# Layer 1's sweep of a hybrid encoder: two units of the gate branch ordered ahead of the recurrence gates, and the last small stores and first row loads re-queued

## The chip, the cores and the metric

The kernel runs on one core of one Trainium2 chip. The metric is device time in microseconds (us) of one execution, as the median of several runs; the profile is that of one more execution. A core has a matrix engine (PE, with its weight loads shown as PEld), a vector engine (DVE), a scalar engine for activation functions (ACT), a general engine (POOL), and a queue engine (SP) that does nothing here but issue transfers (DMA) between the chip's memory and the on-chip memory. Each engine executes its own instructions in a fixed order; an instruction whose operands are not there yet holds up all that stand behind it on that engine. POOL can issue transfers too.

## What is computed

Two layers over 2048 rows of 1024 features. Layer 0 mixes windowed attention and a gated MLP; layer 1 is a bidirectional gated linear recurrence. Only layer 1 is touched:

```
xr, g = split(h @ w_in, 2)                 # 1024 -> 2 x 1024
xr = centred_depthwise_conv(xr, conv_w, conv_b)
y  = rg_lru(xr, ..., reverse=False) + rg_lru(xr, ..., reverse=True)
y  = y * silu(g)
x  = layer_norm(ALPHA * x + gate * (y @ w_out), ln_g, ln_b)

def rg_lru(x, w_a, b_a, w_x, b_x, lam, reverse):
    rec_gate, in_gate = sigmoid(x @ w_a + b_a), sigmoid(x @ w_x + b_x)   # per head, 128 x 128
    log_a = -8 * rec_gate * softplus(-lam)
    a, b = exp(log_a), sqrt(1 - exp(2 * log_a)) * in_gate * x
    h[i] = a[i] * h[i-1] + b[i]            # a scan along the rows, forward or backward
```

## The kernel before

Rows are cut into `NT` = 4 tiles of `C` = 512. All products are made to full float32 accuracy from two halves of each operand, a rounded one and its remainder (`split`, lines 154 and 155: ACT rounds, DVE subtracts), so each product of a 128 x 128 weight block with 512 columns is three matmuls (`mm3`, lines 158 to 160).

**The sweep over the tiles, t = 0 to 3.** For each tile the 1024 recurrence channels and the 1024 gate-branch channels are treated in two halves, s = 0 and 1, of four groups g of 128 channels. For one half:

- `x_job` makes the input branch: `job1` runs `job_cm` over 8 units (a unit is one slice of 128 input features, whose weights are one transfer of 512 KB into a buffer `hl`, eight of which exist), 4 groups x 3 matmuls each, 96 matmuls in all, into 4 PSUM banks `pj` of 5. ACT copies the four results into `X` (line 897).
- `build1(t+1)`, in the second half only, builds the next tile's input (DVE transposes, ACT, DVE, POOL).
- `front` makes, for each group, the convolution on DVE (lines 944 and 947), its split, four gate products of three matmuls into PSUM banks `pm` (weights `hg`, line 953), the activations on ACT, and the scans on DVE (lines 994, 1007, 1014).
- `g_job` makes the gate branch: again 8 units, 96 matmuls, into 4 banks `pj`, copied by ACT (line 918).
- `back` multiplies the two. For t < 3 its results go to memory as rows `a_d`, `b_d`, `f_d`, `g_d`, `u_d`, `v_d`, since the backward scan of a tile needs the tile behind it. For t = 3 they are used at once (`y3`), and the first two columns of each group are stored to `y_d` (line 1040, 8 stores in all), because they belong to the tile before.

**The seam.** After the sweep, the output product of tile 3 is made from `y3`: `part_out` (96 matmuls for each half n of the output columns) into all eight PSUM banks, `ps3`. Meanwhile `load_y(2)` fetches the stored rows of tile 2 and finishes its backward recurrence, eight slices k: for even k the tiles `at`, `bt`, `ft`, `gt` (line 1106), a scan (1113), a sum on POOL (1117), a product (1118); for odd k `ut`, `vt` and one or two corrections by the carry `cr` (1127); then the split into `hi` and `lo` that PE multiplies. The two columns from `y_d` are loaded into the same tiles (line 1130). `residual_tile` loads four tiles `z` of 512 KB, the residual rows of tile 3 (line 1144); line 1164 adds `ps3` to them, which frees the PSUM banks for tile 2's output product, and `finish` normalises them (`norm_rows`, lines 614 to 624). Tiles 1 and 0 follow in the same way.

The loads of the seam go into tiles of the pool `outp`, which is laid over the pool `rnn` of the sweep (`ra`, `T`, `ii`, `G`, `hg`): a load waits for the last use of whatever lay in its place. In a pool, tiles are placed in the order in which they are first allocated. SP issues all of these loads and, before the change, the `y_d` stores. In the program each transfer of SP's queue also waits until the one eight places before it has landed.

**What sets the order.** The text of the program is not the order on the engines: a planner orders each engine's instructions beforehand. At any moment it takes, among the instructions whose operands it believes ready, the one that comes first in the text (evictions marked `high_priority` first of all). The order that it finds is then fixed.

Of the kernel before, what the change touches and what calls it, by code (L numbers as in the profile page):

```python
# [17 lines left out]
D = 1024  # L18
KD = D // 128
C = 512  # L20
NT = S // C
# [8 lines left out]
NEL = 5  # L30
PE_FROM = 14
XH = 1
XB = 2


# [18 lines left out]
def kernel(  # L54
# [27 lines left out]
    nc = tc.nc  # L82
# [5 lines left out]
    store = nc.sync.dma_start  # L88
# [24 lines left out]
    y_d = dram.tile([128, KD, 2], F32, name="y_d")  # L113
# [125 lines left out]
    for i in range(2):  # L239
        nc.gpsimd.dma_start(out=vrow0[24 + 8 * i:32 + 8 * i].rearrange("k (a q) -> k a q", a=4),  # L240
                            in_=ada_b[1, i * D:i * D + D].rearrange("(a k q) -> k a q", a=4, q=32))
# [4 lines left out]
    ps = bank(px, "px")  # L246
# [22 lines left out]
    ps = bank(px, "px")  # L269
# [26 lines left out]
    ps = bank(px, "px")  # L296
# [246 lines left out]
    hT = load_hT(0)  # L543
# [40 lines left out]
    def banks():  # L584
        if turn is None:
            return [bank(pj, "pj") for _ in range(4)]
        r = []
        for _ in range(4):
            r.append(bank(*((pja, "pja"), (px, "px"), (pjb, "pjb"))[turn[0] % 6 // 2]))
            turn[0] += 1  # L590
        return r

    def job_cm(unit, hT):
        ps = banks()
        for k in range(KD):
            hl = unit(k)
            for i in range(4):
                sl = slice(i * 128, i * 128 + 128)
                mm3(ps[i], hl[:, 0, sl], hl[:, 1, sl], hT[0][k], hT[1][k], k == 0, k == KD - 1)
        return ps  # L600
# [37 lines left out]
    for g in range(2):  # L638
        wr = bp.tile([128, 4, 128], F32, tag="wsr", bufs=1, name="wsr")
        load(out=wr, in_=ev_sg_w[0, 4 * g:4 * g + 4].rearrange("g p q -> p g q"))  # L640
        ps = bank(pm, "pm")
# [6 lines left out]
    ps = bank(pm, "pm")  # L648
# [111 lines left out]
    def build1(t):  # L760
        hT = ([], [])
        for k2 in range(4):
            hi, lo = act_pair()
            if k2 % XH == 0:
                xp = tp.tile([128, 16, 64 * XH], F32, tag="xp", bufs=XB, name="xp")
                for a in range(4):
                    f0 = 256 * a + 64 * k2
                    load(out=xp[32 * a:32 * a + 32],
                         in_=x1_d[t * C:t * C + C, f0:f0 + 64 * XH].rearrange("(c i) f -> i c f", i=32))
            for j in range(2):  # L770
# [73 lines left out]
    for t in range(NT):  # L844
        y = sgate(t, hT)
        for m in mods.get(t, []):
            modulation(Ring(bp, bp, "aw", 2, 2), (pm, "pm"), "aw", *m, gate=gates[m[0]])
        hT = load_hT(t + 1) if t + 1 < NT else build1(0)
# [30 lines left out]
    def unit1(i):  # L879
        hl = cp.tile([128, 2, C], F32R, tag="hl", bufs=8, name="hl")  # L880
        nc.sync.dma_start(out=hl.bitcast(F32), in_=w_d[i])
        return hl

    def job1(hT, c0):
        return job_cm(lambda k: unit1(c0 // C * KD + k), hT)

    def span(t):
        j0 = 2 if t == 0 else 0
# [2 lines left out]
    def x_job(t, hT, s):  # L891
        X = []
        for i, p in enumerate(job1(hT, s * C)):
            g = 4 * s + i
            xt = el("X", 5, w=520)
            with tc.high_priority():
                act(out=xt[:, 4:516], in_=p, func=AF.Copy)
            nc.gpsimd.tensor_copy(xt[:, 0:4], halo_x[:, g, :])
            if t == NT - 1:
                nc.gpsimd.memset(xt[:, 516:518], 0.0)  # L900
            else:
                nc.gpsimd.tensor_copy(halo_x[:, g, :], xt[:, 512:516])
            X.append(xt)
        return X

    state = {"last": [], "pend": []}

    def g_job(t, hT, s):
        G = []
        for i, p in enumerate(job1(hT, D + s * C)):  # L910
            g = 4 * s + i
            gt = el("G", 5)
            src = gt[:, 2:514]
            if t == NT - 1:
                src = p
            else:
                with tc.high_priority():
                    act(out=src, in_=p, func=AF.Copy)
            sg = el("sg", 2, w=C)
            r = act(out=sg, in_=src, func=AF.Tanh, scale=0.5)  # L920
            if t < NT - 1:
                after(r, state["last"])
                state["pend"].append(r)
            stt(out=gt[:, 2:514], in0=sg, scalar=1.0, in1=src, op0=ALU.add, op1=ALU.mult)
            nc.gpsimd.tensor_copy(gt[:, 0:2], halo_g[:, g, :])
            if t < NT - 1:
                nc.gpsimd.tensor_copy(halo_g[:, g, :], gt[:, 512:514])
            G.append(gt)
        return G
# [94 lines left out]
    def back(t, s, res, G):  # L1024
        j0, W = span(t)
        w = slice(j0, j0 + W)
        tok = slice(t * C - 2 + j0, t * C - 2 + j0 + W)
        for i in range(4):
            g = 4 * s + i
            if t < NT - 1 and g % 2 == 0:  # L1030
                store(out=g_d[:, g, tok], in_=G[i][:, w])
                continue
            y, A = res[i]
            stt(out=y[:, w], in0=y[:, w], scalar=0.5, in1=G[i][:, w], op0=ALU.mult, op1=ALU.mult)
            if t < NT - 1:
                store(out=u_d[:, g // 2, tok], in_=y[:, w])
                stt(out=A[:, w], in0=A[:, w], scalar=0.5, in1=G[i][:, w], op0=ALU.mult, op1=ALU.mult)
                store(out=v_d[:, g // 2, tok], in_=A[:, w])
                continue
            store(out=y_d[:, g, :], in_=y[:, 0:2])  # L1040
            if i % 2 == 0:
                yp = act_pair()
            split(yp[0][:, i % 2], yp[1][:, i % 2], y[:, 2:514])
            y3[0].append(yp[0][:, i % 2])
            y3[1].append(yp[1][:, i % 2])

    for t in range(NT):
        if t < NT - 1:
            for s in range(2):
                X = x_job(t, hT, s)  # L1050
                if s == 1:
                    nxt = build1(t + 1)
                f = front(t, s, X)
                back(t, s, f, g_job(t, hT, s))
            hT = nxt
        else:
            X0 = x_job(t, hT, 0)
            f0 = front(t, 0, X0)
            X1 = x_job(t, hT, 1)
            f1 = front(t, 1, X1)  # L1060
            sf.close()
            back(t, 0, f0, g_job(t, hT, 0))
            G1 = g_job(t, hT, 1)
# [32 lines left out]
        tt(out=cr[:, t], in0=first_a[:, t + 1], in1=cr[:, t + 1], op=ALU.mult)  # L1096
        tt(out=cr[:, t], in0=cr[:, t], in1=first_h[:, t + 1], op=ALU.add)

    def load_y(t):
        y = ([], [])  # L1100
        n = C if t < NT - 2 else C - 2
        c0 = t * C

        def fetch(tag, src, k):
            p = op.tile([128, C], F32, tag=tag, bufs=2, name=tag)
            load(out=p[:, 0:n], in_=src[:, k, c0:c0 + n])  # L1106
            return p

        for k in range(KD):
            if k % 2 == 0:  # L1110
                at, bt, ft, gt = (fetch(tag, src, k) for tag, src in (("at", a_d), ("bt", b_d), ("ft", f_d), ("gt", g_d)))
                h = bt[:, 0:n]
                nc.vector.tensor_tensor_scan(out=h[:, ::-1], data0=at[:, 0:n][:, ::-1], data1=h[:, ::-1],  # L1113
                                             initial=carry_b[:, t + 1, k:k + 1], op0=ALU.mult, op1=ALU.add)
                if t > 0:
                    nc.gpsimd.tensor_copy(carry_b[:, t, k:k + 1], bt[:, 0:1])
                nc.gpsimd.tensor_tensor(out=ft[:, 0:n], in0=ft[:, 0:n], in1=h, op=ALU.add)
                stt(out=ft[:, 0:n], in0=ft[:, 0:n], scalar=0.5, in1=gt[:, 0:n], op0=ALU.mult, op1=ALU.mult)
                if t == NT - 2 or k < 4:
                    hi, lo = act_pair()  # L1120
                else:
                    hi, lo = (op.tile([128, 2, C], F32R, tag="act2", bufs=8, name=nm) for nm in ("ahi", "alo"))
            else:
                ft, vt = (fetch(tag, src, k // 2) for tag, src in (("ut", u_d), ("vt", v_d)))
                for u, q0, q1 in ((t, 0, C - 2), (t + 1, C - 2, C)):
                    if u < NT - 1:
                        stt(out=ft[:, q0:q1], in0=vt[:, q0:q1], scalar=cr[:, u, k // 2:k // 2 + 1],  # L1127
                            in1=ft[:, q0:q1], op0=ALU.mult, op1=ALU.add)
            if n < C:
                load(out=ft[:, n:C], in_=y_d[:, k, :])  # L1130
            split(hi[:, k % 2], lo[:, k % 2], ft)
            y[0].append(hi[:, k % 2])
            y[1].append(lo[:, k % 2])
        return y
# [6 lines left out]
    def residual_tile(t, b):  # L1141
        r = t * C + b * 128
        z = op.tile([128, D], F32, tag="z", bufs=6, name="z")
        load(out=z, in_=x1_d[r:r + 128, :])
        return z

    zt = [residual_tile(NT - 1, b) for b in range(4)]
    g_bc = op.tile([128, D], F32, name="g_bc1")
    b_bc = op.tile([128, D], F32, name="b_bc1")
    y2 = load_y(NT - 2)  # L1150
    for k in range(4, KD):
        for n in range(2):
            part_out(ps3[n], wo[n][k], k)
# [14 lines left out]
    zt = [residual_tile(NT - 2, b) for b in range(4)]  # L1168
    for n in range(2):
        cs = slice(n * C, n * C + C)  # L1170
        ps = banks() if n == 0 else [bank(pj, "pj")] + [bank(pm, "pm") for _ in range(3)]
# [8 lines left out]
    for t in range(NT - 3, -1, -1):  # L1180
        y = load_y(t)
        for b0, n in ((0, 0), (0, 1), (2, 0), (2, 1)):
            for b in (b0, b0 + 1):
# [4 lines left out]
                ps = bank(pj, "pj") if cnt % 8 < 5 else bank(pm, "pm")  # L1188
# [36 lines left out]
```

## Time and profile before

| | us |
|---|---|
| median of 3 runs | 1558.17 (1556.07 to 1564.16) |
| the profiled execution | 1562.55 |
| its span, first to last instruction | 1560.8 |
| PE busy | 1481.5 |
| DVE busy | 1188.0 |
| ACT busy | 783.5 |
| POOL busy | 405.1 |

The profiled execution stands 4.38 us above the median. Its span was run at a mean granted PE clock of 0.984 of full speed. Durations below are from it. Layer 0 ends, and layer 1's sweep begins, at about 898 us of the span; the seam lies at 1376 to 1450 us.

In rows of the timeline the columns are: start in us, duration in us, engine, line, operation, tiles written and read, shape, count, and in brackets how long the engine had been idle and what ended that. A row with a count covers several neighbouring instructions, from the first one's start to the last one's end. "SPq" rows are SP issuing transfers.

### The profile page before, as it was taken

How to read it: one execution, taken by the hardware profiler on the slowest of the kernel's cores; microseconds unless marked ns; L12 is line 12 of the kernel's file. 1: busy time of each engine (PE TensorE's matmuls, PEld its weight loads, DVE VectorE, ACT ScalarE, POOL GpSimd, SP SyncE). 2: the span in 40 equal slices, each digit the busy share in tenths (PEclk: the TensorE clock that was granted, in tenths of full speed). 3: DMA queues.
4: the chain of work that ended last, by engine and by line, in shares of the span. 5: the costliest groups of instructions: out<-in, count | busy, mean ns of one | idle time of the engine just before them, and what ended most of it. 6: DMA issues, size and time to landing. Idle time of an engine off the chain costs nothing. (4 is left out here: it accounts for less than half of the span.)

```text
span 1560.8 us, 22092 instructions
## 1 busy us (share of the span) xinstructions
PE 1481.5 (95%) x7096; PEld 1185.4 (76%) x7096; DVE 1188.0 (76%) x2180; ACT 783.5 (50%) x1470; POOL 405.1 (26%) x488
## 2 busy tenths in 40 slices
PE   7999999989999999999999999999999999987997
PEld 3887777657777777788887777787777788876886
DVE  4599889745769558976776774987987877789996
ACT  4677767542523332343243327499498486851100
POOL 1023233211005000300120232534645523114321
PEclk9999999999999999999999999999999999998999
DMA  9357776849798989988795699788778667439862
GB/s 346 133 170 219 223 198 187 266 131 298 231 293 302 256 252 300 314 268 266 262 298 177 191 246 294 220 267 282 220 239 288 219 214 237 139 146 340 284 202 88
DMA packets 209211, 370.91 MB, mean 238 GB/s; under 512 B 56616, under 2 KB 103620, under 8 KB 209096
## 3 DMA queue, kind: packets, MB, share of 16 engines
q1 hardware_dynamic: 202344, 354.53, 71.1%
q0 software_dynamic: 6752, 14.98, 3.7%
q8 instruction: 56, 0.92, 0.3%
q14 instruction: 59, 0.48, 0.1%
HBM read 261.96 MB, written 85.97 MB: 223 GB/s over the span
## 5 line engine op out<-in xcount | busy, mean ns | idle before, releaser
L154 ACT ACTIVATE hl<-raw 128x512 fp32r<-128x512 f32 x192 | 118.7, 627 | 224.7 <-DMA raw<-in_ev_w_in_dram 139.0
L158 PE MATMUL pj<-ahi,hl 128*128 128x512 f32 x512 | 200.7, 394 | 1.1 <-DVE gz L753 1.1
L159 PE MATMUL pj<-alo,hl 128*128 128x512 f32 x512 | 201.3, 393 | 0.0
L160 PE MATMUL pj<-ahi,hl 128*128 128x512 f32 x512 | 200.8, 394 | 0.0
L155 DVE TENSOR_TENSOR hl<-raw,hl 128x512 fp32r<-128x512 f32 x192 | 131.9, 696 | 74.3 <-ACT hl L154 74.1
L150 POOL TENSOR_SCALAR rstd<-mv 128x1 f32<-128x1 f32 x32 | 27.4, 857 | 401.6 <-DVE mv L616 289.9
L158 PEld LDWEIGHTS pj<-ahi,hl 128*128 128x128 f32 x512 | 97.4, 190 | 22.2 <-DVE gz L753 1.5
L159 PEld LDWEIGHTS pj<-alo,hl 128*128 128x128 f32 x512 | 97.0, 189 | 20.6
L160 PEld LDWEIGHTS pj<-ahi,hl 128*128 128x128 f32 x512 | 97.0, 189 | 20.6
L465 POOL DMA_DIRECT2D P<-T x112 | 62.4, 566 | 178.9 <-DVE nm L430 77.2
L158 PE MATMUL pj<-wqh,hhi 128*128 128x256 f32 (+1 forms) x256 | 88.3, 349 | 2.5 <-ACT hhi L154 1.7
L430 DVE CUSTOM_DVE_ANT_0 P<-psc,mask,nsink 128x384 f32<-128x384 f32 (+1 forms) x128 | 73.9, 595 | 21.7 <-PE psc L429 21.4
L154 ACT ACTIVATE phl<-praw 128x512 fp32r<-128x512 f32 x56 | 35.4, 632 | 108.2 <-DMA praw<-in_od_w_in_dram 56.6
L159 PE MATMUL pj<-wql,hhi 128*128 128x256 f32 (+1 forms) x256 | 87.9, 344 | 0.0
L160 PE MATMUL pj<-wqh,hlo 128*128 128x512 f32 (+1 forms) x256 | 85.3, 345 | 1.4 <-DVE hlo L155 1.4
L977 DVE SCALAR_TENSOR_TENSOR ii<-ii,xc 128x1024 f32<-128x1024 f32 (+2 forms) x32 | 40.6, 1270 | 58.7 <-ACT ii L971 58.7
L433 ACT ACTIVATE P<-P,nm 128x384 f32<-128x384 f32 (+1 forms) x128 | 76.4, 601 | 11.6 <-DVE nm L430 11.4
L777 POOL TENSOR_TENSOR alo<-hm,ahi 128x512 fp32r<-128x512 f32 x32 | 49.7, 1559 | 119.2 <-DVE hm L776 102.7
L947 DVE SCALAR_TENSOR_TENSOR xc<-X,vcol,xc 128x512 f32<-128x512 f32 (+2 forms) x96 | 77.3, 840 | 0.3
L158 PE MATMUL pm<-xhi,hg 128*128 128x512 f32 (+3 forms) x160 | 56.1, 365 | 13.4 <-ACT xhi L154 6.4
L155 DVE TENSOR_TENSOR phl<-praw,phl 128x512 fp32r<-128x512 f32 x56 | 39.1, 699 | 35.4 <-ACT phl L154 32.1
L775 ACT ACTIVATE ahi<-hm,shift,scale 128x512 fp32r<-128x512 f32 x32 | 25.2, 812 | 75.0 <-DVE hm L774 67.1
(304 smaller groups left out, 4319.2 us busy)
## 6 DMA issues: line engine op xcount, KB each, us to landing
hl<-w_d SPq DMA_DIRECT2D x128, 512.0 KB, 4.8
raw<-in_ev_w_in_dram SPq DMA_DIRECT2D x128, 256.0 KB, 3.9
w_d<-phl SPq DMA_DIRECT2D x40, 512.0 KB, 4.7
aw<-in_ada_w_dram SPq DMA_DIRECT2D x32, 512.0 KB, 6.8
hg<-w_d SPq DMA_DIRECT2D x32, 512.0 KB, 4.0
P<-T SPq DMA_DIRECT2D x104, 96.0 KB, 4.7
P<-T POOLq DMA_DIRECT2D x104, 96.0 KB, 4.2
aw<-in_ada_w_dram SPq DMA_DIRECT2D x8, 1024.0 KB, 7.8
```

Source lines behind the costliest of these rows:

```text
L150: nc.gpsimd.tensor_scalar(out=dst, in0=src, scalar1=mul, scalar2=EPS, op0=ALU.mult, op1=ALU.add)
L154: act(out=hi, in_=src, func=AF.Copy)
L155: tt(out=lo, in0=src, in1=hi.bitcast(F32), op=ALU.subtract)
L158: nc.tensor.matmul(ps, lhsT=ahi, rhs=bhi, start=first, stop=False)
L159: nc.tensor.matmul(ps, lhsT=ahi, rhs=blo, start=False, stop=False)
L160: nc.tensor.matmul(ps, lhsT=alo, rhs=bhi, start=False, stop=last)
L430: nc.vector.tensor_tensor_reduce(out=p[:, g, 0:W], in0=ps[:, 0:W], in1=mask[:, m0:m0 + W], scale=-0.125, scalar=nsink[:, h:h + 1], op0=ALU ...
L433: act(out=p[:, g, 0:W], in_=p[:, g, 0:W], func=AF.Exp, scale=-1.0, bias=nm[:, h:h + 1], accum_out=rs[:, h:h + 1])
L465: dma.dma_start(out=pv[32 * r:32 * r + 32, 0:nb, i], in_=T[32 * i:32 * i + 32, 0:nk].rearrange("p (j r) m -> p r j m", r=4)[:, r])
L777: nc.gpsimd.tensor_tensor(out=lo[:, j], in0=h, in1=hi[:, j].bitcast(F32), op=ALU.subtract)
L947: stt(out=xc[:, w], in0=xt[:, j0 + j:j0 + j + W], scalar=vcol1[:, 8 * j + g:8 * j + g + 1], in1=xc[:, w], op0=ALU.mult, op1=ALU.add)
L977: stt(out=ii[i][:, :, w], in0=ii[i][:, :, w], scalar=1.0, in1=xc[:, None, w].to_broadcast([128, 2, W]), op0=ALU.add, op1=ALU.mult)
```

## The change

Three edits. First, `g_job`'s first `HEAD` = 2 units (24 of 96 matmuls) are written between `x_job` and `build1`/`front` for t < 3; the other six stay behind `front`. Second, the `y_d` stores are issued by POOL instead of SP. Third, tile 3's residual rows `z` are loaded after the first two slices of tile 2's rows instead of before all of them, and the tiles `g_bc`, `b_bc` are allocated after `load_y`.

```
--- before.py
+++ after.py
@@ -30,6 +30,7 @@
 NEL = 5
 PE_FROM = 14
 XH = 1
+HEAD = 2
 XB = 2
 
 
@@ -590,9 +591,10 @@
             turn[0] += 1
         return r
 
-    def job_cm(unit, hT):
-        ps = banks()
-        for k in range(KD):
+    def job_cm(unit, hT, part=range(KD), ps=None):
+        if ps is None:
+            ps = banks()
+        for k in part:
             hl = unit(k)
             for i in range(4):
                 sl = slice(i * 128, i * 128 + 128)
@@ -881,8 +883,8 @@
         nc.sync.dma_start(out=hl.bitcast(F32), in_=w_d[i])
         return hl
 
-    def job1(hT, c0):
-        return job_cm(lambda k: unit1(c0 // C * KD + k), hT)
+    def job1(hT, c0, part=range(KD), ps=None):
+        return job_cm(lambda k: unit1(c0 // C * KD + k), hT, part, ps)
 
     def span(t):
         j0 = 2 if t == 0 else 0
@@ -905,9 +907,9 @@
 
     state = {"last": [], "pend": []}
 
-    def g_job(t, hT, s):
+    def g_job(t, hT, s, ps=None):
         G = []
-        for i, p in enumerate(job1(hT, D + s * C)):
+        for i, p in enumerate(job1(hT, D + s * C, range(0 if ps is None else HEAD, KD), ps)):
             g = 4 * s + i
             gt = el("G", 5)
             src = gt[:, 2:514]
@@ -1037,7 +1039,7 @@
                 stt(out=A[:, w], in0=A[:, w], scalar=0.5, in1=G[i][:, w], op0=ALU.mult, op1=ALU.mult)
                 store(out=v_d[:, g // 2, tok], in_=A[:, w])
                 continue
-            store(out=y_d[:, g, :], in_=y[:, 0:2])
+            nc.gpsimd.dma_start(out=y_d[:, g, :], in_=y[:, 0:2])
             if i % 2 == 0:
                 yp = act_pair()
             split(yp[0][:, i % 2], yp[1][:, i % 2], y[:, 2:514])
@@ -1048,10 +1050,11 @@
         if t < NT - 1:
             for s in range(2):
                 X = x_job(t, hT, s)
+                ps = job1(hT, D + s * C, range(HEAD))
                 if s == 1:
                     nxt = build1(t + 1)
                 f = front(t, s, X)
-                back(t, s, f, g_job(t, hT, s))
+                back(t, s, f, g_job(t, hT, s, ps))
             hT = nxt
         else:
             X0 = x_job(t, hT, 0)
@@ -1096,7 +1099,7 @@
         tt(out=cr[:, t], in0=first_a[:, t + 1], in1=cr[:, t + 1], op=ALU.mult)
         tt(out=cr[:, t], in0=cr[:, t], in1=first_h[:, t + 1], op=ALU.add)
 
-    def load_y(t):
+    def load_y(t, between=None):
         y = ([], [])
         n = C if t < NT - 2 else C - 2
         c0 = t * C
@@ -1107,6 +1110,8 @@
             return p
 
         for k in range(KD):
+            if k == 2 and between is not None:
+                between()
             if k % 2 == 0:
                 at, bt, ft, gt = (fetch(tag, src, k) for tag, src in (("at", a_d), ("bt", b_d), ("ft", f_d), ("gt", g_d)))
                 h = bt[:, 0:n]
@@ -1144,10 +1149,10 @@
         load(out=z, in_=x1_d[r:r + 128, :])
         return z
 
-    zt = [residual_tile(NT - 1, b) for b in range(4)]
+    zt = []
+    y2 = load_y(NT - 2, lambda: zt.extend(residual_tile(NT - 1, b) for b in range(4)))
     g_bc = op.tile([128, D], F32, name="g_bc1")
     b_bc = op.tile([128, D], F32, name="b_bc1")
-    y2 = load_y(NT - 2)
     for k in range(4, KD):
         for n in range(2):
             part_out(ps3[n], wo[n][k], k)
```

More of the change, by code (lines that the diff above doesn't have):

```diff
@@ L32 @@
 XH = 1
+HEAD = 2
 XB = 2
@@ L591, in banks, with job_cm @@
         return r
-    def job_cm(unit, hT):
-        ps = banks()
-        for k in range(KD):
+    def job_cm(unit, hT, part=range(KD), ps=None):
+        if ps is None:
+            ps = banks()
+        for k in part:
             hl = unit(k)
@@ L882, in unit1, with job1 @@
         return hl
-    def job1(hT, c0):
-        return job_cm(lambda k: unit1(c0 // C * KD + k), hT)
+    def job1(hT, c0, part=range(KD), ps=None):
+        return job_cm(lambda k: unit1(c0 // C * KD + k), hT, part, ps)
     def span(t):
@@ L906, with g_job @@
     state = {"last": [], "pend": []}
-    def g_job(t, hT, s):
+    def g_job(t, hT, s, ps=None):
         G = []
-        for i, p in enumerate(job1(hT, D + s * C)):
+        for i, p in enumerate(job1(hT, D + s * C, range(0 if ps is None else HEAD, KD), ps)):
             g = 4 * s + i
@@ L1039, in back @@
                 continue
-            store(out=y_d[:, g, :], in_=y[:, 0:2])
+            nc.gpsimd.dma_start(out=y_d[:, g, :], in_=y[:, 0:2])
             if i % 2 == 0:
@@ L1050 @@
                 X = x_job(t, hT, s)
+                ps = job1(hT, D + s * C, range(HEAD))
                 if s == 1:
@@ L1053 @@
                 f = front(t, s, X)
-                back(t, s, f, g_job(t, hT, s))
+                back(t, s, f, g_job(t, hT, s, ps))
             hT = nxt
@@ L1097, with load_y @@
         tt(out=cr[:, t], in0=cr[:, t], in1=first_h[:, t + 1], op=ALU.add)
-    def load_y(t):
+    def load_y(t, between=None):
         y = ([], [])
@@ L1109, in load_y @@
         for k in range(KD):
+            if k == 2 and between is not None:
+                between()
             if k % 2 == 0:
@@ L1145, in residual_tile @@
         return z
-    zt = [residual_tile(NT - 1, b) for b in range(4)]
+    zt = []
+    y2 = load_y(NT - 2, lambda: zt.extend(residual_tile(NT - 1, b) for b in range(4)))
     g_bc = op.tile([128, D], F32, name="g_bc1")
     b_bc = op.tile([128, D], F32, name="b_bc1")
-    y2 = load_y(NT - 2)
     for k in range(4, KD):
```

## The prediction, made before the change was run

> **What bounds the kernel now.** I read the page first, then who PE waited for in layer 1, then the timeline around the longest wait.
>
> ```profile
> PE 1481.5 (95%) x7096; PEld 1185.4 (76%) x7096; DVE 1188.0 (76%) x2180; ACT 783.5 (50%) x1470; POOL 405.1 (26%) x488
> ```
>
> PE is busy for 95% of the span, so a change that leaves the number of matmuls alone can only win PE's idle time or its slow time. The waits of PE between 895 and 1440 us say where that idle time is (total, times, longest):
>
> ```profile
> PE pj L158 <- ACT ahi L154: 8.2, 1, 8.2
> PE pm L158 <- ACT xhi L154: 6.4, 3, 2.2
> ```
>
> One wait of 8.2 us stands out. Three of about 2.1 us are those of the gates for the split convolution (`xhi`), one per tile. PE's timeline around the large one:
>
> ```profile
> 1402.21 0.39 PE L158 MATMUL pm<-wo,ahi 128*128 128x512 f32 x1
> ...
> 1404.25 0.39 PE L158 MATMUL pj<-wo,ahi 128*128 128x512 f32 x1
> ...
> 1407.65 0.39 PE L158 MATMUL pm<-wo,ahi 128*128 128x512 f32 x1
> ...
> 1409.46 0.39 PE L160 MATMUL pm<-wo,alo 128*128 128x512 f32 x1
> 1418.03 0.80 PE L158 MATMUL pj<-hl,ahi 128*128 128x512 f32 x1 [8.17 <-ACT ahi L154]
> ...
> 1422.44 0.39 PE L158 MATMUL pm<-hl,ahi 128*128 128x512 f32 x1
> ...
> 1443.57 1.19 PE L160 MATMUL pj<-wo,alo 128*128 128x512 f32 x4 [0.30 <-DVE alo L155]
> ```
>
> The first and the third row are 24 matmuls apart: 5.44 us, 0.227 us each, PE's undisturbed pace. Tile 3's product ends at 1409.85, and PE stands idle for 8.17 us until tile 2's first slice is split. Then it is slow: ten matmuls take 1418.03 to 1422.44, 4.41 us where 2.27 would do, another 2.14 us. The windows show the granted clock (columns: length; busy time and count of PE, PEld, DVE, ACT and POOL; clock; DMA share; GB/s):
>
> ```profile
> 1388.00:1390.00 2.00, 2.00 (x11) 1.65 (x10) 2.00 (x2) 0.00 (x0) 0.00 (x0) 1.00 1.03 422
> ...
> 1394.00:1396.00 2.00, 2.00 (x10) 1.65 (x9) 2.00 (x2) 0.00 (x0) 1.68 (x1) 1.00 0.02 8
> ...
> 1398.00:1400.00 2.00, 2.00 (x9) 1.24 (x7) 1.93 (x6) 0.65 (x2) 0.51 (x1) 1.00 0.04 1
> ...
> 1410.00:1412.00 2.00, 0.00 (x0) 0.00 (x0) 0.80 (x1) 0.00 (x0) 0.00 (x0) 1.00 0.90 285
> 1412.00:1414.00 2.00, 0.00 (x0) 0.00 (x0) 2.00 (x4) 0.00 (x0) 1.44 (x2) 0.54 0.98 299
> ...
> 1418.00:1420.00 2.00, 1.97 (x5) 1.61 (x6) 2.00 (x4) 0.00 (x0) 0.84 (x2) 0.50 0.97 279
> ```
>
> The seam thus costs 8.17 + 2.14 = 10.3 us. The same windows show its cause: from 1394 to 1400 the DMA is idle, although 3.5 MB are about to be wanted (1.5 of rows, 2 of `z`). SP's timeline says why:
>
> ```profile
> 1381.99 4.56 SPq L1079 DMA_DIRECT2D wo<-wo_d  x8
> 1397.58 2.30 SPq L1040 DMA_DIRECT2D y_d<-T  x2
> 1399.94 1.94 SPq L1144 DMA_DIRECT2D z<-x_d  x4
> 1402.05 0.32 SPq L1106 DMA_DIRECT2D at<-a_d  x1
> ...
> 1403.79 1.42 SPq L1106 DMA_DIRECT2D gt<-g_d  x1
> ```
>
> After the last weights, at 1386.55, SP reaches the store of the seventh group and waits 11 us for its product, then for the eighth's, before it issues any load. The 2 MB of `z` go ahead of the rows. The chain from there to PE:
>
> ```profile
> 1398.85 0.69 DVE L1034 SCALAR_TENSOR_TENSOR T<-T,G 128x514 f32<-128x514 f32 x1
> 1400.24 0.69 DVE L155 TENSOR_TENSOR alo<-T,ahi 128x512 fp32r<-128x512 f32 x1
> 1405.13 0.69 DVE L1164 SCALAR_TENSOR_TENSOR z<-z,pj 128x512 f32<-128x512 f32 x1 [4.20 <-PE pj L160]
> 1407.15 0.69 DVE L1164 SCALAR_TENSOR_TENSOR z<-z,pj 128x512 f32<-128x512 f32 x1 [1.33 <-PE pj L160]
> 1411.20 1.28 DVE L1113 TENSOR_TENSOR_SCAN bt<-at,carry_b,bt 128x510 f32<-128x510 f32 x1 [1.46 <-DMA bt<-b_d]
> 1416.63 0.68 DVE L1118 SCALAR_TENSOR_TENSOR ft<-ft,gt 128x510 f32<-128x510 f32 x1
> 1417.34 0.63 ACT L154 ACTIVATE ahi<-ft 128x512 fp32r<-128x512 f32 x1 [1.16 <-DVE ft L1118]
> ```
>
> DVE has 4.20 + 1.33 + 1.46 = 6.99 us of idle time from the last split (ends 1400.93) to the first scan, which waits for `bt`; that is the transfer that ends last.
>
> **The stores (edit 2).** Eight issues leave SP and come to POOL. The last two waited at the head of SP's queue; behind them now stand the seam's loads, and these become free to go at 1386.55 instead of 1399.94. What else can hold them is their place: `outp` lies over `rnn`, whose last use is the split that ends at 1400.93. So the first row is issued between 1386.55 and 1400.93. I take the early end for most of them, since `at`, `bt`, `ft` are now the first tiles of their pool, where the weights `hg` lay, and the sweep's last gates are long done, whereas only two of the four `T` in `rnn` are busy until 1400. The transfers then fall into the empty DMA time. On POOL an issue costs what this row says:
>
> ```profile
> L465 POOL DMA_DIRECT2D P<-T x112: 536/545/732, 85.1 to 310.7; - x112
> ```
>
> Eight times 0.55 to 0.73 us is 4.4 to 5.8 us of POOL, which is 26% busy. Behind a waiting store on POOL stands at most the next sum of two scans, whose successor in `y3` PE first needs at 1404.25, three us later than it is ready: I take 0, and as the bounds 0 and 1.4 us, the longest issue and one product (0.73 + 0.69).
>
> The Trainium skill, "Trainium Kernel Development and Optimization", section Key Constraints, speaks against this edit: transfers of all issuing engines share the same DMA engines, and spreading them saves no more than issue time. By that rule the sum would be the two stores' issue time alone, under 1 us. The rows disagree on what is spent: SP's 11 us are a wait ahead of an issue, not an issue.
>
> **Rows before z (edit 3).** Eight transfers of 1.5 MB now precede the 2 MB of `z`. What waits for `z` is line 1164, and for it the PSUM banks of tile 2's product, all eight being `ps3`. The chain that ended last gives the landing of `gt`, and the source view of line 1144 how long a `z` takes:
>
> ```profile
> 1403.79 8.54 DMA gt<-g_d
> ```
>
> ```profile
> DMA to landing us min/median/max: 3.7/6.6/8.4
> ```
>
> From the first issue at 1399.94 to 1412.33, 3 MB took 12.4 us. Started at 1386.55 (the weights still fill the DMA until 1394), all 3.5 MB are in by about 1394 + 14 = 1408 even at that rate; the third and fourth `z` can wait for the last two `T`, until some 1402, and land by 1408.6 with the median of 6.6. Line 1164 cannot start before PE's banks end, 1405.1 to 1409.85, so `z` costs 0 to 1 us; I take 0.
>
> **What is late next.** Slice 0 and slice 1 fit into DVE's idle time after 1400.93 (scan, product, two splits and a correction, which I put at a product: 1.28 + 0.68 + 2 x 0.69 + 0.68 = 4.0 us), so PE can go on at 1409.85 without idling. But DVE is then the rival bound:
>
> ```profile
> 1412.00:1444.00 32.00, 25.68 (x103) 20.79 (x104) 32.00 (x41) 4.42 (x7) 15.79 (x16) 0.84 0.98 335
> ```
>
> It is busy for all 32 us, and PE's fifth slice waited for it (the 0.30 at 1443.57), so PE has no slack there. DVE can run ahead by its 6.99 us of idle time, of which I leave about 1 us unusable; PE wants to run ahead by 10.3. With the same order on DVE, 10.3 - 6.0 = 4.3 us come back as stalls. In that stretch lies tile 3's normalisation, of which this group is a part:
>
> ```profile
> L623 DVE SCALAR_TENSOR_TENSOR z<-z,mv,g_bc 128x1024 f32<-128x1024 f32 (+1 forms) x33 | 40.4, 1233 | 0.1
> ```
>
> Four such passes of 1.23 us are 4.9 us; if the planner puts them behind the slices, nothing comes back. I take 1.3, nearer to nothing: slice 4 needs the buffers of slice 0, which are now free 10 us earlier, so it competes with the normalisation from the start, and it comes first in the text.
>
> The Trainium skill, "TensorE: Matmul & The Clock Gate", Part 1, has the clock halved after an idle window of about 3.4 us and restored after as long a busy one. The trace agrees: full at 1410 to 1412, 0.54 in the next 2 us, full again 4.4 us after the restart. By that rule short stalls, 1.3 or 4.3 us in pieces, would lose no clock, and the sum by it is the same.
>
> **The head (edit 1).** It orders 24 matmuls, 5.44 us, before the gates. The planner already does that, since the gates' operands are not there. Last eviction of X, then the first gates, for a first half, a later first half and a second half (there with G's evictions too):
>
> ```profile
> 919.14 2.58 ACT L897 ACTIVATE X<-pj 128x512 f32<-128x512 f32 x4 [29.03 <-PE pj L160]
> 930.44 0.85 PE L158 MATMUL pm<-xhi,hg 128*128 128x510 f32 x3
> ```
>
> ```profile
> 1037.16 0.63 ACT L897 ACTIVATE X<-pj 128x512 f32<-128x512 f32 x1
> 1048.16 0.85 PE L158 MATMUL pm<-xhi,hg 128*128 128x512 f32 x3
> ```
>
> ```profile
> 1094.51 2.04 ACT L897 ACTIVATE X<-pj 128x512 f32<-128x512 f32 x4
> 1117.67 0.96 PE L158 MATMUL pm<-xhi,hg 128*128 128x512 f32 x3 [2.10 <-ACT xhi L154]
> 1118.86 2.04 ACT L918 ACTIVATE G<-pj 128x512 f32<-128x512 f32 x4
> ```
>
> The distances are 8.7, 10.4 and 21.1 us, all above 5.44; in the second half the whole of G is done before the first gate. The head changes no order here, and the loads of its units go out as before, when X's buffers come free. It cannot cure the 2.1 us either: PE has run out of G there, and DVE is late. I take 0, between -2 (one such wait gone by a shifted order) and +2 (one more).
>
> **The sum.** -8.17 (idle) - 2.14 (slow clock) + 1.3 (DVE) + 0 (POOL) + 0 (`z`) + 0 (head) = -9.0 us on the profiled 1562.55: 1553.5. The profiled execution lies 4.4 us above the median, and I take the same 9.0 off the median: 1549.2.
>
> **The rivals.** A measurement of this kernel tells about 0.5% from no change, 7.8 us.
> - *DVE takes PE's place*, the 4.3 us above: gain 6.0, 1552.2. For it: DVE at 32 of 32 us. Against it: the 4.9 us that can move.
> - *The places hold the rows* until 1400.93. From the first issue to slice 0's being ready, `bt` first, was 1417.97 - 1402.05 = 15.9 us with `z` in the way; without the 2 MB (5 us at the 422 GB/s of the first window above) it is 11 to 13, so PE restarts near 1413: gain about 4 to 5, 1553.9. Against it: the order in which tiles are placed.
> - *Only issue time is saved*: the loads are held by something that the rows don't show, start as late as now, and the gain is the two stores' issues, at most 2 x 0.32 us (as the issue of `at`), 1557.5. Against it: nothing but the store stands between the weights and `z` on SP. The Trainium skill's Key Constraints, as told above, would have it so.
> - *Slower: the head delays the gates.* Place: the six halves with t < 3. Price: 5.44 us each, since DVE and ACT, which set the pace of `front`, start that much later; at all six 32.6 us, less the seam's 9.0: 1581.8. It decides where the gates' operands are ready less than 5.44 us after X; the nearest distance that I read is 8.7.
>
> **How the numbers follow.** The forecast (gain 7.8 to 12) has 0.56, DVE 0.17, the places 0.13, issue time 0.08, the head 0.06. Faster by over 0.5% is the first, 0.56; within 0.5% the next three, 0.38; slower 0.06. The range goes from 1545.5 (gain 12.7: all of the seam and one `xhi` wait) to 1558, which leaves out the head and the edges of the others, some 0.13. Both ends of the terms for POOL, `z`, DVE and the head lie in it.
>
> **What would show it.** Right: the rows' first issue before 1395 and ahead of `z`, DMA busy at 1394 to 1400, no wait of PE above 2 us at tile 2's first slice, clock at 1.00 throughout the seam; PE's waits for `xhi` unchanged, and the first gates at the same distance from X. Wrong: a new wait of PE for `alo` in the middle of tile 2 (DVE); a first row at 1401 or later (the places); a wait for line 1164 at the first matmuls (`z`); first gates 5 us later relative to X (the head).

## The result, and the profile after

| | before | changed |
|---|---|---|
| median of 8 runs, us | 1559.92 (1556.07 to 1570.07) | 1551.54 (1545.88 to 1558.76) |
| ratio to before | 1 | 0.9941, 95% interval 0.9917 to 0.9965 |
| span of the profiled execution, us | 1560.8 | 1550.4 |
| granted clock, mean | 0.984 | 0.990 |

The medians are 8.4 us apart, 0.5%; the interval of the ratio stands for a gain of 5.5 to 12.9 us. (The ratio on record is not the quotient of the two medians, which would be 0.9946.) The two profiled executions are 10.4 us apart. The busy line of the page after:

```profile
PE 1475.9 (95%) x7096; PEld 1181.1 (76%) x7096; DVE 1186.5 (77%) x2180; ACT 784.2 (51%) x1470; POOL 413.1 (27%) x496
```

PE does the same 7096 matmuls; POOL has eight instructions more, the stores. PE's waits after, over layer 1 (total, times, longest; line numbers have moved by one to five):

```profile
PE pm L159 <- ACT xhi L155: 6.5, 3, 2.2
PE pm L159 <- ACT ra L968: 4.2, 3, 3.2
PE pm L159 <- DMA hg<-w_d: 3.3, 3, 1.3
...
PE pj L159 <- ACT ahi L155: 0.6, 1, 0.6
```

The wait of 8.2 us for `ahi` has become one of 0.6; the three for `xhi` are what they were. SP's timeline shows what let the first one go:

```profile
1383.99 2.22 SPq L1082 DMA_DIRECT2D wo<-wo_d  x5
1386.25 0.44 SPq L1109 DMA_DIRECT2D at<-a_d  x1
...
1393.79 0.32 SPq L1109 DMA_DIRECT2D gt<-g_d  x1
...
1396.05 9.14 SPq L1149 DMA_DIRECT2D z<-x_d  x4
```

The first row goes right behind the last weights, at 1386.25 instead of 1402.05. `gt` is the one that had to wait for its place: SP waited 6.0 us there for a scan (`T`, line 1009). The four `z` are spread over 9.14 us, and SP's waits name what held them, the stores that POOL now issues and that still read the places which `z` is to take:

```profile
SPq L1149 <- DMA y_d<-T: 7.3, 2, 6.6
```

The same windows as before (length; busy time and count of PE, PEld, DVE, ACT, POOL; clock; DMA share; GB/s):

```profile
1394.00:1396.00 2.00, 2.00 (x10) 1.65 (x9) 2.00 (x2) 0.00 (x0) 1.80 (x1) 1.00 0.65 187
...
1410.00:1412.00 2.00, 2.00 (x10) 1.65 (x9) 2.00 (x4) 0.00 (x0) 0.00 (x0) 1.00 1.04 366
...
1412.00:1444.00 32.00, 31.42 (x139) 25.68 (x138) 30.82 (x40) 4.95 (x8) 18.37 (x16) 1.00 1.00 340
```

The DMA, idle at 1394 to 1396 before (share 0.02), now works; the clock stays at 1.00; and in 1412 to 1444 PE does 139 matmuls where it did 103. PE's timeline across the seam, then DVE's:

```profile
1409.58 0.39 PE L161 MATMUL pm<-wo,alo 128*128 128x512 f32 x1
1409.81 0.39 PE L159 MATMUL pj<-hl,ahi 128*128 128x512 f32 x1
...
1421.42 0.50 PE L159 MATMUL pj<-hl,ahi 128*128 128x512 f32 x1 [0.58 <-ACT ahi L155]
```

```profile
1400.35 0.69 DVE L156 TENSOR_TENSOR alo<-T,ahi 128x512 fp32r<-128x512 f32 x1
1400.96 1.27 DVE L1118 TENSOR_TENSOR_SCAN bt<-at,carry_b,bt 128x510 f32<-128x510 f32 x1
...
1406.57 0.68 DVE L1169 SCALAR_TENSOR_TENSOR z<-z,pj 128x512 f32<-128x512 f32 x1
```

The first matmul of tile 2 follows the last of tile 3 by 0.23 us, which is PE's pace. On DVE the first scan now comes straight behind the last split, with no idle time, and slice 0 is split before the first pass of line 1169, so PE never sees it.

**A measure for the seam alone.** The medians scatter by several us, because layer 0 and the sweep do. The time from the end of tile 3's product to the end of the span doesn't. It is the span less the end of the last matmul: 1560.8 - 1409.85 = 150.95 us before, 1550.4 - 1409.97 = 140.43 after, 10.5 us less. The experiments use it beside the medians. Where the seam of before stands, it was 150.95, 150.73 and 150.53 (mean 150.74); where the changed seam stands as it is, 139.92 to 141.06 in eight profiles.

### The profile page after: what moved, and what is told of

It reads as the page before. It is cut to its first block, busy times and chain, and to the rows that moved or that the text cites. A ratio compares the mean times of both kernels' runs of the same rounds, so it can differ in the third digit from the quotient of the medians.

```text
span 1550.4 us, 22105 instructions
## 1 busy us (share of the span) xinstructions
PE 1475.9 (95%) x7096; PEld 1181.1 (76%) x7096; DVE 1186.5 (77%) x2180; ACT 784.2 (51%) x1470; POOL 413.1 (27%) x496
## 5 line engine op out<-in xcount | busy, mean ns | idle before, releaser
L151 POOL TENSOR_SCALAR rstd<-mv 128x1 f32<-128x1 f32 x32 | 32.0, 999 | 409.7 <-DVE mv L618 297.3
L161 PEld LDWEIGHTS pj<-ahi,hl 128*128 128x128 f32 x512 | 96.8, 189 | 20.3
```

Source lines behind the costliest of these rows:

```text
L151: nc.gpsimd.tensor_scalar(out=dst, in0=src, scalar1=mul, scalar2=EPS, op0=ALU.mult, op1=ALU.add)
L161: nc.tensor.matmul(ps, lhsT=alo, rhs=bhi, start=False, stop=last)
```

## The experiments

Theory: the whole gain is the seam's. Two small stores waited at the head of SP's queue, the loads behind them came late, and PE ran dry and cold; the head does nothing. Rivals: the head brings part; one of the two other edits is all; POOL has something to do with it.

| kernel | median, us | ratio to before, 95% interval | last matmul of tile 3 ends, us | span, us | from there to the end, us |
|---|---|---|---|---|---|
| e1 head only | 1562.63 | 1.0002, 0.9988 to 1.0015 | 1410.87 | 1561.6 | 150.73 |
| e2 stores on POOL only | 1560.35 | 0.9976, 0.9960 to 0.9992 | 1411.10 | 1558.6 | 147.50 |
| e3 rows first only | 1560.46 | 0.9969, 0.9952 to 0.9985 | 1414.97 | 1560.4 | 145.43 |
| e4 changed, no head | 1555.32 | 0.9947, 0.9928 to 0.9966 | 1409.61 | 1550.1 | 140.49 |
| e5 stores on ACT | 1554.84 | 0.9950, 0.9933 to 0.9967 | 1410.95 | 1552.9 | 141.95 |
| e6 two stores on POOL | 1555.81 | 0.9948, 0.9930 to 0.9965 | 1419.53 | 1560.4 | 140.87 |
| e7 head of eight | 1552.05 | 0.9922, 0.9899 to 0.9946 | 1403.24 | 1544.3 | 141.06 |
| e8 convolutions in turn | 1574.60 | 1.0087, 1.0064 to 1.0109 | 1439.08 | 1579.0 | 139.92 |
| e9 head of eight again | 1549.47 | 0.9911, 0.9883 to 0.9939 | 1407.90 | 1548.3 | 140.40 |
| e10 changed again | 1555.49 | 0.9943, 0.9922 to 0.9965 | 1417.19 | 1557.6 | 140.41 |
| e11 head of six | 1561.96 | 0.9978, 0.9955 to 1.0002 | 1419.92 | 1560.6 | 140.68 |
| e12 head of eight on before | 1562.08 | 0.9980, 0.9957 to 1.0002 | 1405.67 | 1556.2 | 150.53 |

The kernel before had medians of 1564.01 (beside e1 to e4), 1563.67 (e5 to e8) and 1564.20 us (e9 to e12).

### The three edits one by one (e1 to e4)

**e1, the head alone** (`HEAD = 2` and the split of `job1`, on the kernel before):

> The kernel before with the head alone (edit 1). Theory (the gain is the seam's, through the loads): the head leaves the order of the work as it is, so the time is that of before within 0.3% (1556 to 1564 us), PE waits 8 us at tile 2's first slice as before, and the three waits for xhi stay at 2.1 to 2.2 us. Rival (the head brings part of the 8.4 us): at least 3 us faster than before, and the first gates lie at another distance from X.

PE's timeline at the seam:

```profile
1419.08 0.80 PE L159 MATMUL pj<-hl,ahi 128*128 128x512 f32 x1 [8.21 <-ACT ahi L155]
```

The wait is there as before, 8.21 us, and the ratio is 1.0002. The head also leaves the instructions of all engines in the order they had: the traces of before and of e1 list the same instructions in the same order on every engine, and so do those of the changed kernel and of e4 below. The text asks for 24 matmuls ahead of the gates where the planner puts more anyway. With six units, 72 matmuls, the order does change (e11 below).

**e2, the stores alone:**

```
-            store(out=y_d[:, g, :], in_=y[:, 0:2])
+            nc.gpsimd.dma_start(out=y_d[:, g, :], in_=y[:, 0:2])
```

> The kernel before with the stores on POOL alone (edit 2); z is still loaded ahead of the rows. Theory (store out of SP's way, and places by order of allocation): z is issued from about 1387 us, but the first row tile lies where the last T lies, so at is issued at about 1401 us as before; without the 2 MB of z beside them the rows land 3 to 5 us sooner, PE waits 3 to 5 us in place of 8.2, gain 4 to 6 us (1554 to 1556 us). Rival (the stores' place on SP's queue was all): all of the 8.4 us, PE waits under 1 us. Second rival (places hold everything): gain under 2 us, the wait stays at 7 us or more.

SP's timeline, SP's waits, and PE's timeline:

```profile
1387.67 8.05 SPq L1144 DMA_DIRECT2D z<-x_d  x4
1402.90 0.32 SPq L1106 DMA_DIRECT2D at<-a_d  x1
```

```profile
SPq L1106 <- DMA y_d<-T: 7.0, 1, 7.0
```

```profile
1416.26 0.79 PE L158 MATMUL pj<-hl,ahi 128*128 128x512 f32 x1 [5.16 <-ACT ahi L154]
```

`z` is issued from 1387.67, but the first row at 1402.90, as late as ever. It doesn't wait for the split of the last `T` alone, as I had it, which ended at 1402.17, but for the transfer of the store that reads that `T`, some 0.6 us longer: the store no longer stands ahead of the row in a queue, yet it still sits on the row's place. The gain is 150.74 - 147.50 = 3.2 us in the profile, with a ratio of 0.9976; a wait of 5.16 us is left (my bound was 5), with the half clock behind it.

**e3, the rows first alone** (`load_y(NT - 2, ...)` ahead of `z`, the stores still by SP):

> The kernel before with the rows ahead of z alone (edit 3); the stores still go by SP. Theory: the first row is issued when the eighth store lets SP go, at about 1400 us, 2 us earlier than in before and with no z ahead, so bt lands at about 1406 and slice 0 is split at about 1412 to 1414: PE waits 3 to 5 us, gain 4 to 7 us (1553 to 1556 us). Rival (order of loads was all, the stores cost nothing): all of the 8.4 us, PE waits under 1 us. Second rival (z is missed by line 1164 once it comes last): a new wait of PE for the banks of tile 3's product, and no gain.

SP's and PE's timelines:

```profile
1402.68 2.30 SPq L1040 DMA_DIRECT2D y_d<-T  x2
1405.04 0.42 SPq L1106 DMA_DIRECT2D at<-a_d  x1
...
1409.81 2.46 SPq L1146 DMA_DIRECT2D z<-x_d  x4
```

```profile
1417.10 0.64 PE L158 MATMUL pj<-hl,ahi 128*128 128x512 f32 x1 [2.13 <-DVE z L1166]
```

DVE's timeline ahead of that:

```profile
1410.69 1.28 DVE L1115 TENSOR_TENSOR_SCAN bt<-at,carry_b,bt 128x510 f32<-128x510 f32 x1 [4.67 <-DMA ft<-y_d]
...
1415.66 0.69 DVE L155 TENSOR_TENSOR alo<-ut,ahi 128x512 fp32r<-128x512 f32 x1
1416.27 0.68 DVE L1166 SCALAR_TENSOR_TENSOR z<-z,pj 128x512 f32<-128x512 f32 x1
```

(This sweep ended some 5 us later than that of before, so the clock times are shifted.) The first row goes 0.06 us after the stores. The theory's wait, for the split of slice 0, isn't what ends last: PE waits 2.13 us for line 1166 to free a bank. That looks like the second rival, a `z` that comes too late, but DVE didn't wait for `z`: line 1166 follows the split of slice 1 without idle time. DVE's long wait, 4.67 us, is the one before the first scan, for the rows. With edit 3 slices 0 and 1 stand ahead of line 1166 on DVE, where in before its first passes came ahead of the scan, so rows that come late now hold up line 1166 as well. What was late is the rows, as in the theory, by a path that it didn't name. The gain, 5.3 us in the profile and a ratio of 0.9969, has the size that the theory gave. PE waits once more, 1.25 us, for an `ahi` at 1431.11.

**e4, both without the head:**

> The changed kernel without the head (edits 2 and 3 alone). Theory: the same time as the changed kernel, 1549 to 1554 us, with PE's wait at tile 2's first slice under 1 us and the waits for xhi at 2.1 to 2.2 us. Rival (the head brings part): at least 3 us slower than the changed kernel.

Ratio 0.9947 against the changed kernel's 0.9941, 140.49 us from the product to the end against 140.43. What follows from the four: the head is worth nothing, the stores alone 3.2 us of the seam, the rows alone 5.3, both together 10.2. Each alone leaves a wait above 2 us, and with it the slow clock; only both together get rid of it.

### What takes the stores, and how many of them (e5, e6)

e5 is the changed kernel with `nc.scalar.dma_start` in place of `nc.gpsimd.dma_start`:

> The changed kernel with the eight stores issued by ACT in place of POOL. Theory (what counts is that they leave SP's queue; who takes them is free): the same time as the changed kernel, ratio to before 0.992 to 0.997, rows first issued at about 1386 us, PE's wait at tile 2's first slice under 1 us. ACT splits the same T right behind each store, so a store holds nothing up there. Rival (POOL's own queue is what helps, or ACT pays for the issues): the last two splits of tile 3 come 0.5 to 1.2 us later, and PE waits so much more at tile 3's product or at tile 2's first slice.

SP's waits in 1384 to 1410 us, then PE's timeline:

```profile
SPq L1109 <- DMA y_d<-T: 4.0, 1, 4.0
SPq L1135 <- DMA y_d<-T: 2.7, 1, 2.7
```

```profile
1399.76 0.50 PE L159 MATMUL pj<-wo,ahi 128*128 128x512 f32 x1 [0.37 <-ACT ahi L155]
1423.37 0.50 PE L159 MATMUL pj<-hl,ahi 128*128 128x512 f32 x1 [1.53 <-ACT ahi L155]
```

Ratio 0.9950, nearly all of the gain. PE waits 0.37 us for ACT's split in tile 3's product, ahead of the stretch that the seam's measure takes in. That stretch is 1.5 us longer (141.95 against 140.43): PE waits 1.8 us there for splits, 1.53 of them in one, where the changed kernel has 0.58. The loads of `vt` and of `y_d` wait 6.7 us for these stores, where in the changed kernel it is only `z` that waits for them. The trace tells why: the rule that a transfer waits for the one eight places before it comes from eight semaphores that the transfers take in turn, and those that ACT issues take them from the same eight as SP's. Here `vt` has the semaphore of the seventh store (number 116) and the load of `y_d` that of the eighth (100); in the changed kernel POOL's stores have others (106 and 107). That this makes up the 1.5 us is argued, not shown. So POOL isn't the cause of the gain; in the one profile of each it is the better place by 1.5 us, and the ratios don't tell the two apart.

e6 leaves the first six stores on SP:

```
+            (nc.gpsimd if g >= 6 else nc.sync).dma_start(out=y_d[:, g, :], in_=y[:, 0:2])
```

> The changed kernel with only the stores of the seventh and eighth group on POOL; the first six go by SP as in before. Theory (only the two that wait at the head of SP's queue cost time): the same time as the changed kernel, ratio to before 0.992 to 0.997, rows first issued at 1386 to 1388 us. Rival (all eight have to leave SP, because the earlier ones delay the last weights): rows first issued at 1390 us or later, and 2 us or more of the gain is lost.

```profile
1390.66 0.93 SPq L1042 DMA_DIRECT2D y_d<-T  x2
...
1395.92 0.48 SPq L1109 DMA_DIRECT2D at<-a_d  x1
```

By the clock of its run the first row is at 1395.92, but that whole sweep ended 9.6 us later. Against the end of tile 3's product it goes 1419.53 - 1395.92 = 23.6 us ahead; in the changed kernel 1409.97 - 1386.25 = 23.7. Nothing is lost: two stores of eight cost everything.

### The head, made to bind (e7, e9, e11, e12)

e7 has `HEAD = 8`: all of the gate branch ahead of the gates.

> The changed kernel with all eight units of the gates' branch (96 matmuls, 21.8 us) ordered ahead of the gates, in place of two. Theory (two units cost nothing because the planner runs 43 matmuls or more there anyway; an order beyond that binds): in the three first halves the first gates come 10 to 13 us later after X, in the three second halves, where all 96 stand first already, nothing changes; PE has nothing left to lay beside the gates of the first halves, so it waits there: 10 us or more in all, ratio to the changed kernel 1.006 or more. Rival (the order is free, since DVE and ACT set the pace of the sweep either way): within 0.3% of the changed kernel.

The distance from X to the first gates in the first half, ACT and then PE, first in the changed kernel and then in e7:

```profile
919.83 2.58 ACT L899 ACTIVATE X<-pj 128x512 f32<-128x512 f32 x4 [27.42 <-PE pj L161]
931.13 0.85 PE L159 MATMUL pm<-xhi,hg 128*128 128x510 f32 x3
```

```profile
916.68 2.58 ACT L899 ACTIVATE X<-pj 128x512 f32<-128x512 f32 x4 [27.39 <-PE pj L161]
940.22 0.39 PE L159 MATMUL pm<-xhi,hg 128*128 128x510 f32 x1
```

8.7 us became 21.0, so the order does bind, by as much as expected. But it costs nothing: the ratio is 0.9922, where the theory had 0.6% more than the changed kernel's 0.9941. The rival, that the order is free, held. The kernel was run again, beside the changed kernel:

> The head of eight units once more, with more rounds and beside the changed kernel. The first look was 3 to 4 us faster than the changed kernel, where 10 us slower had been expected. If the gain is real: ratio to before 0.990 to 0.994, 2 to 6 us below the changed kernel of this comparison, no wait of PE for xhi, and 2 to 4 us less of waits between 1340 and 1385 us. If it was the scatter of four runs: ratio within 0.1% of the changed kernel's.

> The changed kernel once more, as the measure for the other three. Ratio to before 0.992 to 0.997; over the profiles the seam was worth 10.4 us, over the medians 8.4: if the difference is scatter, the profiled execution again ends 10 us sooner after tile 3's product than in before (140.4 against 150.9 us), whatever the time of the whole.

e9 had 1549.47 us and e10 1555.49 in the same comparison, 6.0 us apart. Ratios to before: 0.9911 and 0.9922 for the head of eight, 0.9941 to 0.9950 for the five kernels with the changed seam and a head that orders nothing new. (e10 has the seam's measure of the changed kernel again, 140.41.) The intervals of single comparisons overlap, so that it beats the changed kernel is likely rather than shown by the times; that it beats the kernel before is shown. The profiles say more, counted over the same work: the last 1000 matmuls up to the end of tile 3's product take 214.8 to 214.9 us in the three profiles with a head of eight (e7, e9, e12) and 220.6 to 222.6 in the nine with the old order. Some of it is lost earlier in the sweep: over the last 2100 matmuls it is 478.5 to 482.2 us against 482.6 to 488.6. e9's waits of PE in layer 1, and the window with the last tile's gates in the changed kernel and in e9:

```profile
PE pm L159 <- ACT ra L968: 7.3, 5, 2.5
PE pm L159 <- DMA hg<-w_d: 4.1, 2, 3.3
PE pm L159 <- ACT ii L973: 3.3, 7, 1.0
```

```profile
1335.00:1395.00 60.00, 54.20 (x271) 45.60 (x271) 46.47 (x52) 47.20 (x79) 10.51 (x10) 0.97 0.42 154
```

```profile
1335.00:1395.00 60.00, 55.74 (x280) 46.30 (x279) 49.51 (x55) 43.28 (x72) 12.60 (x12) 1.00 0.47 166
```

The waits for `xhi` are gone, others have come, and the totals of the three largest hardly differ (after 6.5 + 4.2 + 3.3 = 14.0, e9 7.3 + 4.1 + 3.3 = 14.7). A part of the gain shows in the last tile, where no head is ordered, though the planner puts its matmuls in another order too: nine matmuls more in the same 60 us, 2 us at PE's pace, at a clock of 1.00 instead of 0.97. The clock falls to half three times in the changed kernel's sweep and once in e9's (the last section has what a fall costs). Two more kernels ask what makes it:

> The changed kernel with six units (72 matmuls, 16.3 us) ahead of the gates. In the trace of the changed kernel at least 43 matmuls (3.6 units) stand there unasked, so six bind, as eight do. If the gain of eight comes from having the first half's gates stand beside the next X instead of beside G, six give part of it: ratio to before between those of the changed kernel and of eight, the waits for xhi shorter than 2.1 us. If it comes from the last unit alone (G's evictions free their banks before the gates want ACT), six give nothing.

> The kernel before with the head of eight units alone, without the stores and without the rows: the seam stays as in before. If the head's gain and the seam's are separate: 2 to 6 us faster than before (ratio 0.996 to 0.9985), PE's wait at tile 2's first slice 8 us as before, no waits for xhi. If the head's gain only exists with the new seam: ratio 1.000 within 0.1%.

Six units are no step on the way from two to eight: 1561.96 us, 6.5 more than the changed kernel beside it, with as good a seam (140.68). The two intervals overlap, so that six are slower is likely rather than shown. One wait for `xhi` is left, of 1.63 us, but the first reading in the expectation, part of the gain, fell; the second, that only the last unit counts, isn't excluded. Eight units on the old seam give 0.9980 with an interval that takes in 1, there is no wait for `xhi`, and PE waits at the seam as ever:

```profile
1413.32 0.79 PE L159 MATMUL pj<-hl,ahi 128*128 128x512 f32 x1 [7.65 <-ACT ahi L155]
```

Its profile has the old seam's measure, 150.53, and the quicker sweep of e7 and e9 (the last 1000 matmuls above). So the seam and the sweep are separate matters in the profiles; its times alone don't show a gain. An order of the gate branch that binds makes another pattern of waits in the sweep. Why eight units gain and six don't stays open.

### Whose are the waits for xhi (e8)

```
+                r = ts(out=xc[:, w], in0=xt[:, w], scalar1=vcol1[:, g:g + 1], scalar2=vcol1[:, 32 + g:33 + g], op0=ALU.mult, op1=ALU.add)
+                after(r, res_c if s == 1 and t < NT - 1 else [])
...
+                    r = stt(out=xc[:, w], in0=xt[:, j0 + j:j0 + j + W], scalar=vcol1[:, 8 * j + g:8 * j + g + 1],
...
+                res_c = [r]; xhi = el("xhi", 2, F32R)
```

The first step of a group's convolution is placed behind the last step of the group before it.

> The changed kernel with the four convolutions of a second half (t < 3) run on DVE one after the other, where they were run interleaved; nothing else is ordered. Theory (the three waits for xhi of 2.1 us are DVE's: it has the first group's convolution ready only with the fourth's): the first xhi is split some 8 us sooner, the three waits of 2.1 to 2.2 us go, gain 3 to 6.5 us over the changed kernel, 1545 to 1549 us. Rival (the wait moves): the sweep's end stays where it is within 1 us, since PE then waits as much for sigmoids, for hg or for G later in the same half.

The first split in a second half, behind X, first in the changed kernel and then in e8 (ACT's timeline):

```profile
980.01 2.04 ACT L899 ACTIVATE X<-pj 128x512 f32<-128x512 f32 x4
1002.37 1.14 ACT L155 ACTIVATE xhi<-xc 128x510 fp32r<-128x510 f32 x2
```

```profile
988.79 2.04 ACT L899 ACTIVATE X<-pj 128x512 f32<-128x512 f32 x4
1005.55 0.63 ACT L155 ACTIVATE xhi<-xc 128x510 fp32r<-128x510 f32 x1 [10.22 <-DVE xc L949]
```

It comes 14.7 us after X in place of 20.3, 5.6 sooner (8 were expected). e8's waits of PE in layer 1, and between 1330 and 1400 us alone:

```profile
PE pm L159 <- ACT ra L968: 16.5, 14, 5.1
...
PE pm L159 <- ACT xhi L155: 2.3, 1, 2.3
```

```profile
PE pm L159 <- ACT ra L968: 9.7, 6, 5.1
```

Two of the three waits for `xhi` go, 4.2 us, and 12.3 us come back as waits for the sigmoids alone (4.2 to 16.5): 1.0087. The rival was right in kind, and far too mild. Over half of the waits for sigmoids lie in the last tile, where the convolutions' order was not touched: the planner, given one order, chose others downstream. So DVE's interleaving does delay the first group, as the theory had it, but taking the waits of 2.1 us out by that alone costs more than they do.

## Why the prediction was right, and where not

The prediction was 1549.2 us with 1545.5 to 1558; measured were 1551.54. Of its gain of 9.0 us the medians show 8.4, the profiles 10.4. That 9.0 lies so near to 8.4 is partly luck: without the term for DVE, which wasn't there, the sum was 10.3, and the interval, 5.5 to 12.9, takes in both. (The gain at the lower end of the range, 12.7, is 12.5 by its own terms, 8.17 + 2.14 + 2.2.)

- **The idle 8.17 us**: gone, as stated, and by the path stated. e4 and e1 show that the two seam edits carry all of it; e6, that it is the two stores at the head of the queue.
- **The clock, 2.14 us**: gone; 1.00 through the seam. 8.17 + 2.14 = 10.3 us is what the seam's measure gave (10.5, and 10.2 between the means of the three profiles with the old seam and the eight with the new). That short stalls lose no clock, as the prediction had it, wasn't put to the test in this seam and doesn't hold elsewhere; the last section has the rows.
- **DVE, +1.3**: the term that was mis-sized. It is about 0. PE's only later wait is the 0.58 at 1421.42, in place of 0.30 before, and DVE had slack again, 30.82 of 32 us. The bound of 0 and the argument for it, passes that can move behind the slices, held; I should have taken the bound. The 4.0 us for slices 0 and 1 left out the sum on POOL, for which DVE waited 1.67 us between scan and product; slice 0 was rounded at 1405.26 even so, 4.5 us before PE wanted it.
- **POOL, 0**: held. e5 shows what the stores cost where the issuing engine has work on the path: PE waits 0.37 us in tile 3's product.
- **z, 0**: held, though its time was off: the third and the fourth wait not for the splits, until 1402, but for the stores that read their places, until 1405 (the 7.3 us shown above). No run shows the price of a late `z`: in e3, which loads it last, line 1166 wasn't held by it, and in e5 DVE waits 0.5 us for one without PE waiting for DVE. In the changed kernel line 1169 runs from 1406.57, behind slice 1's split, and DVE waits for no `z`.
- **The head, 0**: held exactly, since it orders nothing new. But the price of the rival built on it, 5.44 us for each half whose gates start that much later, isn't borne out: in e7 they start 12 us later and cost nothing. e11, with six units, has a median 6.5 us above the changed kernel's, so an order that binds may cost something all the same.
- **Places hold the rows** (4 to 5 us): not in the changed kernel, but it is what e2 is, with 3.2.
- **Only issue time**, the rule of the Trainium skill ("Trainium Kernel Development and Optimization", Key Constraints): refuted as a bound on this edit. e2 moves nothing but the issue of eight stores and gains 3.2 us of the seam; an issue was 0.32 us. The rule speaks of issuing, and here a queue was waiting.

What isn't settled is the difference between 10.4 us in the profiles and the 7.8 to 9.2 us that the five ratios of the changed seam (0.9950 to 0.9941) stand for. Ahead of the seam the scatter is larger than that: the first matmul of the sweep that waits for layer 0 (`gz`) starts between 897.93 and 909.74 us in these profiles, though no kernel differs ahead of it. The intervals take in both values.

## What to carry to other kernels

A small transfer that waits for a late result belongs on a queue on which nothing urgent stands behind it; look for an idle DMA while an in-order queue waits, and price the wait ahead of the issue, not the issue. Moving it off the queue is half of it: as long as it runs, it also holds the place it reads from, so the tiles wanted first should be given places that come free early. A wait that is one of a balanced pattern (here the 2.1 us for `xhi`) is not worth its length: the order that took two of three out (e8) had a median 11 us above that of the kernel before.

## What the runs showed of the hardware

**Half clock after some waits of 2.1 us.** The prediction had short stalls lose no clock. In the changed kernel, two waits of PE for `xhi`, 2.18 and 2.16 us long, came out differently (the columns of the windows are as above):

```profile
1003.03 0.96 PE L159 MATMUL pm<-xhi,hg 128*128 128x510 f32 x3 [2.18 <-ACT xhi L155]
```

```profile
999.24:1002.65 3.41, 1.61 (x8) 0.99 (x6) 3.41 (x6) 1.00 (x2) 1.07 (x2) 1.00 0.72 171
1002.65:1006.07 3.42, 3.04 (x13) 2.53 (x14) 3.42 (x7) 3.42 (x7) 0.11 (x1) 1.00 0.92 321
```

```profile
1117.90 1.00 PE L159 MATMUL pm<-xhi,hg 128*128 128x512 f32 x3 [2.16 <-ACT xhi L155]
```

```profile
1115.29:1118.70 3.41, 1.25 (x6) 0.71 (x5) 3.41 (x6) 2.18 (x4) 0.00 (x0) 1.00 0.97 278
1118.70:1122.11 3.41, 3.41 (x9) 2.63 (x8) 3.41 (x7) 2.43 (x5) 1.92 (x2) 0.50 1.09 294
```

Behind the first the clock stays at 1.00. Behind the second it is 0.50 for 3.41 us, in which PE starts eight matmuls, 1.82 us at its pace: the wait cost another 1.6 us. In e3 the wait of 2.13 us was followed by eight matmuls in 3.43 us, from 1417.10 to 1420.53. But e9's wait of 3.32 us, which ended at 966.32, lost nothing.

The Trainium skill, "TensorE: Matmul & The Clock Gate", Part 1, has the clock drop after an idle window of about 3.4 us that runs freely. The traces agree as to the window. In the trace of before the clock falls at 1002.58, 1118.63, 1234.68, 1371.21 and 1412.17 us; these times are 34, 34, 40 and 12 times 3.413 us apart, and each fall lasts 3.41 us or, at the seam, three times as long. The windows above begin and end at such times. The wait that ended at 1117.90 lies whole in one of them, which is idle for 2.16 of its 3.41 us; the one that ended at 1003.03 leaves its window 1.80 us idle; e9's falls into two, with 1.7 and 1.6 us idle. So it counts how a wait falls on the windows, and not its length alone. A window need not be idle throughout: from 895 to 1440 us in the fourteen traces, each window at full clock in which PE was idle for 1.97 us or more was followed by half clock, none with less than 1.87 us was, and between the two both occur.
